# A planner that knows the array's tilings orders the routing, the mixtures and the last block

## The chip, the cores and the metric

The kernel runs on one core of a Trainium2 chip. The metric is the device time of one execution in microseconds (us), as the median of several runs.

## The reference, cut to what matters

Three residual blocks in float32 on 512 tokens of width 1024 (and, in the first block, 256 context tokens).

```python
# block 1: gated delta rule over 768 tokens, then a mixture of 16 experts
x, ctx = x + gate * gdn_mixer(norm(x), norm(ctx)), ...
x, ctx = x + gate * ec_moe(norm(x)), ctx + gate * ec_moe(norm(ctx))
# block 2: state-space mixer over 512 tokens, then a mixture of 16 experts
x = x + gate * ssd_mixer(norm(x), ...)
x = x + gate * ec_moe(norm(x))
# last block: three mixers side by side, then a gated feed-forward
h = rms_norm(x)
mixed = g0 * s5(h) + g1 * short_conv(h) + g2 * sparse_attention(h)
x = x + mixed @ w_out
x = x + (silu(h2 @ w_gate) * (h2 @ w_up)) @ w_down

def ec_moe(h, w_router, w_gate, w_up, w_down):   # every expert takes its best tokens
    aff = softmax(h @ w_router)
    gate, idx = top_k(aff.T, 2 * n // 16)        # 64 of 512 tokens, 32 of 256 context tokens
    xs = h[idx]
    y = (silu(xs @ w_gate[e]) * (xs @ w_up[e])) @ w_down[e] * gate
    return scatter_add(idx, y)
```

## The kernel before, in words

The kernel is written as a plain program of engine calls, but none of them is issued at once. A recorder (`Rec`) keeps each call with its engine, its operands, the calls it must follow (`preds`) and an estimated time (`cost`). At some dozen places `flush` turns the recorded calls into an order. `schedule` is a list scheduler: it keeps a clock for every engine (`free_at`), and again and again takes, over all engines, the ready call that can start first. Among the first 48 ready calls of an engine (`WINDOW`) the one with the best rank wins unless another starts more than `tol` ns earlier. The rank is the place in the program minus `beta` times the length of the chain that hangs on the call. `flush` runs `schedule` for every pair (`beta`, `tol`) in `trials`, takes the order with the shortest planned span, and issues it. That order is what each engine's queue holds on the chip, the queue of SyncE (SP), which issues all transfers, included. All this happens before the launch.

In the plan, a transfer costs its bytes at 360 per ns and transfers run one after the other. For TensorE the plan before has one row of matmuls, each holding the engine for its own cost. A matmul with 32 stationary columns, which occupies a quarter of the array, costs a quarter of a full one plus 27 ns; that four of them can run beside each other on four column strips, and that strips must be empty before the array is cut in another way, is not in the plan.

Which calls are where:

- First flush: norm of the input and the first part of the modulation (`ada`).
- `gdn`: the whole first mixer, its output projection and the logits of the first routing, one flush.
- `moe`, called with `two` true for the first mixture (tokens and context): one flush for softmax, top-k (`v.max`, `match_replace`), positions and the gather products `xs`, filled with two more rounds of `ada`; then one flush for the 16 experts. In the second mixture (tokens alone) there is a flush more after expert 5, and the preparation of the s5 mixer (`s5_prep`) rides in the rest.
- An expert: gate, up and context products (`eg`, `eu`, `ec`) from weight pieces `we` of 1 MB, each piece a transfer; the activation `eth`, `ct`; its transposes `hT` (tokens) and `hcT` (context); the down products `ey`, `eyc`; splits of the result into two parts (`yh`, `yl`, `ch`, `cl`). For every second expert `combine` spreads two experts' rows over the tokens: a matmul `pb` with 16 rows makes positions, VectorE compares (`pts`, one buffer), eight matmuls `po` follow, and VectorE adds each `po` pair to `X`. For every fourth expert the same is done for the context (`pbc`, `poc`).
- `ssd`: the second mixer (one flush), then its output projection and the second routing's logits (one flush).
- The last block: `s5` with the short convolution, `nsa` (the sparse attention: `sc` scores, `PT` transposes, `po` products with 64 columns, `hid` with 32 columns), `mix_out` and `ffn`, one flush each.

Stationary shapes: `eg`, `eu`, `ec`, `ey`, `eyc` of the first mixture are 128 rows by 32 columns; in the second mixture `eg`, `eu`, `ey` are 128 by 64; `hT`, `po`, `xs` are 128 by 128; `hcT` is 64 by 128; `pb`, `pbc` are 16 by 128. A float32 matmul appears in the trace as two MATMUL instructions; a 128-column one in the split number format as one.

All instructions of the program carry line 304 in the trace, the line of `flush` that issues them, so they are told apart by their tiles.

Of the kernel before, what the change touches and what calls it, by code (L numbers as in the profile page):

```python
# [11 lines left out]
F32 = mybir.dt.float32  # L12
F32R = mybir.dt.float32r
# [39 lines left out]
class Rec:  # L53
# [4 lines left out]
    def __init__(self, nc, tc):  # L58
        self.nc, self.tc = nc, tc
        self.tiles, self.ops = {}, []  # L60
        self.access = {}
        for e in ("tensor", "vector", "scalar", "gpsimd", "sync"):
            setattr(self, e, Proxy(self, e))
        self.free_at = {e: 0.0 for e in ("tensor", "vector", "scalar", "gpsimd", "sync")}
        self.dma_free = 0.0
        self.slot_times = {}
        self.seen = set()
        self.npool = 0
        self.run = None
        self.stacks, self.left = {"left": [], "right": []}, {"left": [], "right": []}  # L70
# [74 lines left out]
    def record(self, i, engine, method, a, k):  # L145
        reads, writes = [], []
        for j, x in enumerate(a):
            if isinstance(x, bass.AP):
                (writes if j == 0 else reads).append(x)
        for key, x in k.items():  # L150
            if isinstance(x, bass.AP):
                (writes if key in self.WRITES else reads).append(x)
        if method == "matmul" and not k.get("start", True):
            reads = reads + [writes[0]]
        preds = set()
        rr = [self.region(x) for x in reads]
        ww = [self.region(x) for x in writes]
        if engine != "tensor":
            rr, ww = ([r if not self.tiles.get(r[0], (0, 0, 0))[2] else (r[0], 0, 128) + r[3:] for r in z] for z in (rr, ww))
        for regs, wr in ((rr, False), (ww, True)):  # L160
            for r in regs:
                for (j, w2, q) in self.access.get(r[0], ()):
                    if (wr or w2) and j != i and q[1] < r[2] and r[1] < q[2] and q[3] < r[4] and r[3] < q[4]:
                        preds.add(j)
        for regs, wr in ((rr, False), (ww, True)):
            for r in regs:
                lst = self.access.setdefault(r[0], [])
                if wr:
                    lst[:] = [t for t in lst if not (r[1] <= t[2][1] and t[2][2] <= r[2] and r[3] <= t[2][3] and t[2][4] <= r[4])]
                lst.append((i, wr, r))  # L170
        if engine == "tensor":
            r = ww[0]
            key = r[0] + "#pe"
            q = (key, r[1] // 32 * 32, -(-r[2] // 32) * 32, 0, 1)
            lst = self.access.setdefault(key, [])
            preds.update(j for j, _, z in lst if j != i and q[1] < z[2] and z[1] < q[2])
            lst[:] = [t for t in lst if not (q[1] <= t[2][1] and t[2][2] <= q[2])]
            lst.append((i, True, q))
        names = {r[0] for r in rr + ww}
        cost = self.cost(engine, method, reads, writes, a, k)  # L180
        if i < len(self.ops):
            o = self.ops[i]
            o["preds"] |= preds
            o["names"] |= names
            o["cost"] += cost
            o["more"].append((method, a, k))
            return
        self.ops.append(dict(e=engine, m=method, a=a, k=k, preds=preds, names=names, cost=cost, psum=any(self.tiles.get(r[0], (0, 0, 0))[2] for r in rr + ww)))

    def cost(self, engine, method, reads, writes, a, k):  # L190
        def free(x):
# [48 lines left out]
    def latency(self, e, f):  # L240
        return self.LATENCY.get((e, f), 150.0)

    def flush(self, trials=((0.0, 30.0),)):

        ops = self.ops
        n = len(ops)
# [48 lines left out]
            t[o["e"]] = t.get(o["e"], 0.0) + (475.0 if "dma" in o["m"] else cost[i])  # L295
        static = succ, order, uses, conc, pos, size, tag, drain, tail, before
        best = min((self.schedule(static, *x) for x in trials), key=lambda r: r[0])
        self.span, self.seq, self.free_at, self.dma_free, times = best
        self.slot_times.update(times)
        self.seen.update(uses)  # L300
        for i in self.seq:
# [5 lines left out]
    def schedule(self, static, beta, tol):  # L307
# [13 lines left out]
        for t, lst in order.items():  # L321
            for nm in lst:
                if nm in self.seen:
                    got.add(nm)
                    slots[t].remove(max(slots[t]))
                    alloc[t].add(pos[nm])
                    nxt[t] = pos[nm] + 1
        npred = [len(o["preds"]) for o in ops]
        ready, end = [0.0] * n, [0.0] * n
        cand = {e: [] for e in free_at}  # L330
# [15 lines left out]
        while len(seq) < n:  # L346
            best = None
            for e, c in cand.items():
                fe = free_at[e]
                eb = None  # L350
                for r in c[: self.WINDOW]:
                    i = by[r]
                    st = max(fe, ready[i])
                    if eb is not None and st >= eb[0] - tol:
                        continue
                    for nm in ops[i]["tiles"]:
                        if nm in got:
                            continue
                        t = tag[nm]
                        if not free(nm) or (pos[nm] != nxt[t] and self.tiles[nm][2] and not drains(nm)):  # L360
                            break
                        st = max(st, min(slots[t]))
                    else:
                        if eb is None or st < eb[0] - tol:
                            eb = (st, r)
                            if st <= fe:
                                break
                if eb is not None and (best is None or eb < best[:2]):
                    best = eb + (e,)
            if best is None:  # L370
                return math.inf, seq, free_at, dma_free, slots
            st, r, e = best
            i = by[r]
            o = ops[i]
            cand[e].remove(r)
            for nm in o["tiles"]:
                if nm in got:
                    continue
                got.add(nm)
                t = tag[nm]  # L380
                slots[t].remove(min(slots[t]))
                alloc[t].add(pos[nm])
                ooo[t].add(pos[nm])
                while nxt[t] in alloc[t]:
                    ooo[t].discard(nxt[t])
                    nxt[t] += 1
            if "dma" in o["m"]:
                free_at[e] = st + 475.0
                dma_free = max(st + 1125.0, dma_free) + o["cost"] / 360.0
                fin = dma_free + 900.0  # L390
            else:
                fin = st + o["cost"]
                free_at[e] = fin
            end[i] = fin
            for nm in o["tiles"]:
                left[nm] -= 1
                if not left[nm]:
                    t = tag[nm]
                    slots[t].append(fin + 100.0)
                    ooo[t].discard(pos[nm])  # L400
            for j in succ[i]:
                npred[j] -= 1
                ready[j] = max(ready[j], fin + self.latency(e, ops[j]["e"]))
                if not npred[j]:
                    bisect.insort(cand[ops[j]["e"]], rank[j])
            seq.append(i)
        return max(end), seq, free_at, dma_free, slots


D = 1024  # L410
# [166 lines left out]
def gdn(K, H, apply, w, ba_w, conv_w, a_log, dt_b, norm_g, scr, bscr, tscr, rscr, side, xc, w_out, gate, route):  # L577
# [7 lines left out]

    nc, tc = K.nc, K.tc
    es = ExitStack()
    K.ring(es, 15)
    per = nc.pool(es, "gdn_per")
    live = nc.pool(es, "gdn_live")  # L590
# [352 lines left out]
            K.mm3(p, wt[:, d, :], last[:, t0:t1], True, True)  # L943
            v.scalar_tensor_tensor(X[:, d, t0:t1], p, gate(z)[:, d:d + 1], sums[d][:, t0:t1], op0=OP.mult, op1=OP.add)
    Rs = route(X, live.tile([128, 3, KT, 32], F32, name="router", tag="o", bufs=1))
    nc.flush(GDN_TRIALS)
    es.close()
    return X, Rs


GDN_TRIALS = ((0.4, 0.0),)
GDN_K = 128
GDN_V = 128

# [182 lines left out]
def moe(K, X, ws, regions, gate, routed, keep_next, gain, fill, side):  # L1137
# [153 lines left out]
    if two:  # L1291
        P0 += [places(0, 4, NE), places(1, 0, NE)]
        for k in range(KT):
            gather(k, P0)
            if 0 < k < 4:
                gates(*P0[k - 1])
    nc.flush(((0.0, 0.0),) if two else ((0.6, 30.0),))
    es.close()

    es = ExitStack()  # L1300
# [146 lines left out]
def ssd(K, H, apply, w, wz, w_dt, conv_w, conv_b, a_log, dt_b, d_skip, norm_g, w_out, gate, keep, scr, rscr, side, route):  # L1447
# [6 lines left out]
    nc = K.nc  # L1454
    v, s, g_, pe = nc.vector, nc.scalar, nc.gpsimd, nc.tensor
    es = ExitStack()
    K.ring(es, 18)
    per = nc.pool(es, "ssd_per")
    ssq = per.tile([128, TX], F32, name="ssq")
# [207 lines left out]
    for c in range(6):  # L1667
        scaled(c, Pair(low[:, 2 * c, :], low[:, 2 * c + 1, :]))
    nc.flush(((0.3, 30.0), (0.1, 0.0), (0.6, 0.0)))
    es1.close()  # L1670
    es2 = ExitStack()
    o = nc.pool(es2, "ssd_o")
# [23 lines left out]
        v.scalar_tensor_tensor(u, p, gate[:, d:d + 1], Rs, op0=OP.mult, op1=OP.mult)  # L1696
        v.tensor_tensor(X[:, d, 0:512], u, X[:, d, 0:512], op=OP.add)
    Rs = route(X, o.tile([128, 3, KT, 32], F32, name="router"))
    nc.flush(((0.6, 30.0), (0.8, 30.0), (0.8, 120.0)))
    es2.close()  # L1700
    es.close()
    return X, Rs
# [501 lines left out]
def mix_out(K, H, I, y5, yc, ya, keep, gain):  # L2204
# [41 lines left out]
        s.activation(H.hi[:, k, :], X[:, k, 0:512], AF.Copy, scale=gain[:, k:k + 1])  # L2246
        v.scalar_tensor_tensor(H.lo[:, k, :], X[:, k, 0:512], gain[:, k:k + 1], H.hi[:, k, :].bitcast(F32), op0=OP.mult, op1=OP.subtract)
    Rs = norm_stats(K, X, REGIONS_X)
    nc.flush(((0.6, 30.0),))
    es.close()  # L2250
    return X, Rs

# [4 lines left out]
def ffn(K, X, H, R, I, out):  # L2257
# [21 lines left out]
    for d in range(8):  # L2279
# [3 lines left out]
            K.mm3(p, wt[:, k, :], ht[k], k == 0, k == 21)  # L2283
        v.tensor_tensor(X[:, d, 0:512], p, X[:, d, 0:512], op=OP.add)
        nc.sync.dma_start(out[:, d, :], X[:, d, 0:512])
    nc.flush(((0.6, 30.0),))
    es.close()


def block2(K, X, Rs, I, scr, par, e_par, uscr, keep, out):  # L2290
# [21 lines left out]
    for half in range(2):  # L2312
        s5(K, H, I, y5[2 * half:2 * half + 2], scr, par[half], uscr, half, *pools)
        conv(2 * half)
        conv(2 * half + 1)
    nc.flush(((0.0, 30.0), (0.0, 60.0), (0.3, 60.0), (0.6, 60.0)))
    e2.close()
    e_par.close()
    b = nc.pool(e1, "b2a")
    ya = [b.tile([128, 512], F32, name=f"ya{i}") for i in range(4)]  # L2320
    e3 = nsa(K, H, I, ya)
    nc.flush(((1.0, 30.0),))
    e3.close()
    X, Rs = mix_out(K, H, I, y5, yc, ya, keep, ng[:, 1, :])
    e1.close()
# [195 lines left out]
```

## Time and profile before

| | |
|---|---|
| time, median of 3 runs | 3677.41 us (3665.22 to 3683.21) |
| profiled execution: its time | 3660.83 us |
| profiled execution: span from first to last instruction | 3659.1 us |
| TensorE busy | 3359.7 us, 92% of the span |
| VectorE, ScalarE, GpSimd busy | 51%, 32%, 15% |
| HBM traffic | 644.26 MB read, 21.30 MB written |
| mean granted TensorE clock | 0.971 |

The share of busy TensorE time is an upper figure: a strip of the array that works alone counts as a busy TensorE. Matmuls overlap in the records, so the time that one of them takes from the engine is read from the distance of starts, not from its own duration.

### The profile page before, as it was taken

The numbers are of one execution on the slowest core, as the hardware profiler recorded it, in microseconds if no ns is written. First come the engines' busy times: TensorE is split into PE (matmuls) and PEld (weight loads), VectorE is DVE, ScalarE is ACT, GpSimd is POOL, SyncE is SP. The second block draws the span as 40 slices with busy tenths as digits, with TensorE's granted clock in tenths as the row PEclk, the third lists the DMA queues.
The fourth block names the chain that finished last, engine by engine and source line by source line (L and its number), as shares of the span: only waits on it lengthen the run. The fifth ranks groups of instructions, "written<-read, shape, count | busy, mean of one in ns | idle before, by whom it ended". The sixth has DMA issues, their size and how long they took to land. (4 is left out here: it accounts for less than half of the span.)

```text
span 3659.1 us, 55424 instructions
## 1 busy us (share of the span) xinstructions
PE 3359.7 (92%) x21505; PEld 2255.5 (62%) x21505; DVE 1848.2 (51%) x4086; ACT 1181.0 (32%) x2518; POOL 555.4 (15%) x753
## 2 busy tenths in 40 slices
PE   7987979899999999899999879888879999999999
PEld 4776765666344444677877654332257658878887
DVE  4666755562223222778778542452164564445542
ACT  3354543423111111355555321120032353333331
POOL 0646544301000000013222010010011000000000
PEclk9999989899999999999999889999999999999999
DMA  5522227455888888354241359999962303333322
GB/s 188 160 60 56 74 65 230 155 188 197 342 312 311 335 317 315 111 147 133 93 141 53 140 220 401 362 368 421 420 143 81 119 1 98 96 100 92 96 87 87
DMA packets 251652, 669.21 MB, mean 183 GB/s; under 512 B 72156, under 2 KB 85612, under 8 KB 202236
## 3 DMA queue, kind: packets, MB, share of 16 engines
q1 hardware_dynamic: 251388, 665.66, 51.4%
q8 instruction: 169, 2.77, 0.3%
q14 instruction: 95, 0.78, 0.1%
HBM read 644.26 MB, written 21.30 MB: 182 GB/s over the span
## 5 line engine op out<-in xcount | busy, mean ns | idle before, releaser
L304 DVE TENSOR_TENSOR wl<-w,wh 128x512 fp32r<-128x512 f32 (+3 forms) x452 | 323.1, 717 | 458.8 <-PE fu L304 68.0
L304 ACT ACTIVATE wh<-w 128x512 fp32r<-128x512 f32 (+3 forms) x500 | 307.7, 622 | 675.2 <-PE fu L304 120.7
L304 PE MATMUL eg<-we,xs 128*32 128x512 f32 (+1 forms) x1536 | 371.5, 596 | 8.3 <-DMA we<-moe_w 7.2
L304 PE MATMUL eu<-we,xs 128*32 128x512 f32 (+1 forms) x1536 | 322.3, 595 | 7.4 <-DMA we<-moe_w 7.4
L304 PE MATMUL ey<-we,hTs 128*32 128x512 f32 (+1 forms) x1536 | 295.1, 601 | 17.2 <-ACT hTs L304 9.0
L304 PE MATMUL px<-H,wl 128*128 128x512 f32 (+1 forms) x768 | 269.3, 372 | 21.4 <-DVE wl L304 21.3
L304 PE MATMUL px<-H1l,wh 128*128 128x512 f32 (+1 forms) x768 | 267.3, 364 | 0.0
L304 PE MATMUL px<-H,wh 128*128 128x512 f32 (+1 forms) x768 | 266.1, 370 | 0.5 <-ACT wh L304 0.3
L304 PE MATMUL ec<-we,xs 128*32 128x512 f32 x1024 | 235.2, 594 | 0.0
L304 DVE TENSOR_TENSOR yl<-ey,yh 64x512 fp32r<-64x512 f32 x64 | 44.1, 689 | 337.8 <-ACT yh L304 337.3
L304 PEld LDWEIGHTS eg<-we,xs 128*32 128x32 f32 (+1 forms) x1536 | 96.3, 118 | 140.2 <-issue 103.9
L304 POOL TENSOR_TENSOR wl<-w,wh 128x512 fp32r<-128x512 f32 x48 | 64.6, 1346 | 761.7 <-DVE H1l L304 658.1
L304 DVE SCALAR_TENSOR_TENSOR eth<-eth,eg 128x512 f32<-128x512 f32 x32 | 22.0, 687 | 310.8 <-ACT eth L304 310.8
L304 PEld LDWEIGHTS eu<-we,xs 128*32 128x32 f32 (+1 forms) x1536 | 91.9, 119 | 141.1 <-issue 105.8
L304 PEld LDWEIGHTS ey<-we,hTs 128*32 128x32 f32 (+1 forms) x1536 | 97.3, 120 | 127.6 <-issue 61.8
L304 PEld LDWEIGHTS px<-H,wl 128*128 128x128 f32 x768 | 143.1, 192 | 43.8 <-DVE wl L304 26.2
L304 ACT ACTIVATE eth<-eg 128x512 f32<-128x512 f32 x32 | 19.1, 595 | 462.0 <-PE eg L304 404.7
L304 PEld LDWEIGHTS px<-H,wh 128*128 128x128 f32 x768 | 144.3, 192 | 25.0 <-issue 6.1
L304 PEld LDWEIGHTS px<-H1l,wh 128*128 128x128 f32 x768 | 142.9, 192 | 18.6 <-issue 1.3
L304 PE MATMUL eyc<-we,hcTs 128*32 128x256 f32 x1024 | 140.9, 379 | 0.0
L304 POOL TENSOR_TENSOR D<-D,x 48x30 f32<-48x30 f32 (+14 forms) x240 | 133.7, 557 | 18.3
L304 POOL TENSOR_TENSOR x<-D 48x30 f32<-48x30 f32 (+14 forms) x240 | 127.0, 529 | 59.4 <-DVE D L304 41.5
(1040 smaller groups left out, 7564.1 us busy)
## 6 DMA issues: line engine op xcount, KB each, us to landing
we<-moe_w SPq DMA_DIRECT2D x384, 1024.0 KB, 7.9
w<-ada_w SPq DMA_DIRECT2D x192, 256.0 KB, 5.2
w<-w_gu SPq DMA_DIRECT2D x88, 256.0 KB, 3.4
w<-gdn_w SPq DMA_DIRECT2D x64, 256.0 KB, 3.1
w<-ssd_w SPq DMA_DIRECT2D x64, 256.0 KB, 3.1
w<-w_mix SPq DMA_DIRECT2D x48, 256.0 KB, 2.7
w<-w_dn SPq DMA_DIRECT2D x40, 256.0 KB, 2.6
w<-ssd_wz SPq DMA_DIRECT2D x32, 256.0 KB, 2.6
```

The costliest lines, as they stand in the source:

```text
L304: getattr(getattr(self.nc, o["e"]), m)(*a, **k)
```

## The change

Nothing is added to or taken from the program that the chip runs; only the order of the calls is planned anew. `Rec.array` gives for each TensorE call its tiling (stationary rows and columns, rounded up to 32, 64 or 128), its place in that tiling, and the time that it holds that place. While the flag `plain` is false, `schedule` keeps the tiling that the array is in (`mode`), the time until which each place is held (`held`) and the time when all are done (`drained`). A call of the same tiling can start when its place is free, 7 ns behind the call before it; a call of another tiling starts 94 ns (`SWITCH`) after everything has drained. This state is handed from flush to flush. `plain` is set in `gdn` up to its end and in the first flush of `ssd`, which keep the plan as it was. The other flushes use fifteen pairs, `beta` in 0, 0.2, 0.4, 0.6, 1.0 with `tol` in 0, 30, 90, where they had one to four pairs before.

```diff
+    SWITCH = 94.0
+    @staticmethod
+    def array(method, a):
...
+        size = lambda x: 32 if x <= 32 else 64 if x <= 64 else 128
+        lhs, n = a[1], free(a[2])
+        rows, cols = size(lhs.ap[0][1]), size(free(lhs))
...
+        two = lhs.dtype == F32 and method != "transpose"
+        d = (2 if two else 1) * n / 2.4 + (13.5 if lhs.dtype == F32R else 4.0)
...
+        return (rows, cols), (r0 // rows, c0 // cols), (2 if two else 1) * d
...
-    def flush(self, trials=((0.0, 30.0),)):
+    TRIALS = tuple((b, t) for b in (0.0, 0.2, 0.4, 0.6, 1.0) for t in (0.0, 30.0, 90.0))
+    def flush(self, trials=TRIALS):
...
                     st = max(fe, ready[i])
+                    if e == "tensor" and not self.plain:
+                        tiling, place, _ = ops[i]["pe"][0]
+                        st = max(st, held.get(place, 0.0) if tiling == mode else drained + self.SWITCH)
...
+            elif e == "tensor" and not self.plain:
+                fin = at = st
+                for tiling, place, t in o["pe"]:
+                    if tiling != mode:
+                        if mode is not None:
+                            at = max(at, drained + self.SWITCH)
+                        mode, held = tiling, {}
+                    at = max(at, held.get(place, 0.0))
+                    held[place] = at + t
+                    drained = max(drained, at + t)
+                    fin = max(fin, at + t)
+                    at += 7.0
+                free_at[e] = max(at, held[place]) if mode == (128, 128) else at
...
 # gdn
+    nc.plain = True
...
-    nc.flush(GDN_TRIALS)
+    nc.flush(((0.4, 0.0),))
+    nc.plain = False
...
 # moe, first flush
-    nc.flush(((0.0, 0.0),) if two else ((0.6, 30.0),))
+    nc.flush()
...
 # ssd: plain for its first flush; then
-    nc.flush(((0.6, 30.0), (0.8, 30.0), (0.8, 120.0)))
+    nc.flush()
...
 # last block: mix_out and ffn (before: one pair each), s5 (four pairs), nsa
-    nc.flush(((0.6, 30.0),))
+    nc.flush()
...
-    nc.flush(((0.0, 30.0), (0.0, 60.0), (0.3, 60.0), (0.6, 60.0)))
+    nc.flush()
...
-    nc.flush(((1.0, 30.0),))
+    nc.flush()
```

## Rows read from the trace of the kernel before

**Rows 1.** Stretches of the span: busy us (x instructions), granted clock, DMA share, GB/s.

```profile
0.00:815.00 815.00, 701.30 (x5364) 530.20 (x5364) 488.38 (x1308) 338.13 (x802) 336.44 (x569) 0.94 0.43 132
815.00:870.00 55.00, 51.56 (x510) 40.99 (x512) 24.76 (x58) 30.27 (x80) 12.15 (x13) 0.97 0.06 20
870.00:1500.00 630.00, 615.16 (x5543) 276.37 (x5536) 179.97 (x387) 93.69 (x189) 0.29 (x2) 1.00 0.81 314
1500.00:2124.00 624.00, 570.89 (x3137) 475.98 (x3136) 460.45 (x901) 301.09 (x642) 137.48 (x98) 0.96 0.36 114
2124.00:2672.00 548.00, 473.09 (x2451) 194.56 (x2446) 201.95 (x453) 91.05 (x176) 46.02 (x34) 0.97 0.92 371
2672.00:2818.00 146.00, 126.32 (x816) 102.14 (x816) 81.73 (x155) 41.72 (x68) 23.02 (x38) 0.95 0.48 120
...
2893.00:3013.00 120.00, 111.20 (x575) 61.52 (x575) 80.56 (x235) 59.62 (x185) 0.00 (x0) 0.98 0.10 35
3013.00:3659.00 646.00, 637.04 (x2808) 519.57 (x2808) 286.97 (x439) 200.75 (x331) 0.00 (x0) 0.99 0.31 93
```

**Rows 2.** One slice inside the second mixture, same view and columns.

```profile
2561.00:2653.00 92.00, 77.46 (x334) 24.02 (x330) 16.83 (x26) 7.73 (x13) 0.00 (x0) 1.00 1.01 421
```

**Rows 3.** DMA issues of the page: the expert weights, KB each, us to landing.

```profile
we<-moe_w SPq DMA_DIRECT2D x384, 1024.0 KB, 7.9
```

**Rows 4.** TensorE groups, 870 to 1500 us: busy, mean ns, idle before.

```profile
L304 PE MATMUL ey<-we,hTs 128*32 128x512 f32 x1024 | 174.2, 594 | 6.0 <-DMA we<-moe_w 5.3 <-ACT hTs L304 0.8
L304 PE MATMUL eyc<-we,hcTs 128*32 128x256 f32 x1024 | 140.9, 379 | 0.0
L304 PE MATMUL po<-pts,yh 128*128 128x512 f32 x64 | 23.0, 420 | 1.0 <-ACT yh L304 0.9
```

**Rows 5.** TensorE in order of time, first mixture: start, us, operation, [idle before].

```profile
891.25 0.65 PE L304 MATMUL hT<-cst,eth 128*128 128x128 f32 x4
891.83 0.62 PE L304 MATMUL eg<-we,xs 128*32 128x512 f32 x1
...
893.68 0.46 PE L304 MATMUL hcT<-cst,ct 64*128 64x64 f32 x4
894.07 1.06 PE L304 MATMUL ey<-we,hTs 128*32 128x512 f32 x6
...
1095.55 1.04 PE L304 MATMUL ey<-we,hTs 128*32 128x512 f32 x8
1096.41 0.61 PE L304 MATMUL eyc<-we,hcTs 128*32 128x256 f32 x8
1096.84 0.60 PE L304 MATMUL eg<-we,xs 128*32 128x512 f32 x2
...
1097.90 1.21 PE L304 MATMUL po<-pts,yh 128*128 128x512 f32 x4
1099.33 1.20 PE L304 MATMUL po<-pts,yl 128*128 128x512 f32 x4 [0.21 <-DVE yl L304]
1100.46 0.39 PE L304 MATMUL pb<-posr,slp 16*128 16x512 bf16 x1
...
1498.55 0.39 PE L304 MATMUL poc<-pts,ch 128*128 128x256 f32 x1
```

**Rows 6.** VectorE group, 870 to 1500 us, same columns as rows 4.

```profile
L304 DVE SCALAR_TENSOR_TENSOR X<-po,mod,X 128x512 f32<-128x512 f32 x64 | 43.6, 743 | 1.1 <-PE po L304 0.7
```

**Rows 7.** TensorE in order of time, attention of the last block.

```profile
2893.45 1.05 PE L304 MATMUL hid<-w,A 128*32 128x256 f32 x4
2894.43 0.91 PE L304 MATMUL sc<-kz,qp 128*128 128x384 f32 x2
...
2947.33 1.07 PE L304 MATMUL po<-PT,vt 128*64 128x512 f32 x2
2948.34 1.20 PE L304 MATMUL PT<-cst,P 128*128 128x128 f32 x9
...
3003.30 2.78 PE L304 MATMUL po<-PT,vt 128*64 128x256 f32 x12
```

More of the change, by code (lines that the diff above doesn't have):

```diff
@@ L66, in __init__ @@
         self.slot_times = {}
+        self.array_at = None, {}, 0.0
+        self.plain = False
         self.seen = set()
@@ L180, in record @@
         cost = self.cost(engine, method, reads, writes, a, k)
+        pe = self.array(method, a) if engine == "tensor" else None
         if i < len(self.ops):
@@ L186, in record, with free @@
             o["more"].append((method, a, k))
+            o["pe"].append(pe)
             return
-        self.ops.append(dict(e=engine, m=method, a=a, k=k, preds=preds, names=names, cost=cost, psum=any(self.tiles.get(r[0], (0, 0, 0))[2] for r in rr + ww)))
+        self.ops.append(dict(e=engine, m=method, a=a, k=k, preds=preds, names=names, cost=cost, pe=[pe], psum=any(self.tiles.get(r[0], (0, 0, 0))[2] for r in rr + ww)))
+    SWITCH = 94.0
+    @staticmethod
+    def array(method, a):
+        def free(x):
+            n = 1
+            for s, c in x.ap[1:]:
+                n *= c
+            return n
+        size = lambda x: 32 if x <= 32 else 64 if x <= 64 else 128
+        lhs, n = a[1], free(a[2])
+        rows, cols = size(lhs.ap[0][1]), size(free(lhs))
+        r0, c0 = (x.offset // x.ap[0][0] % 128 if x.ap[0][0] else 0 for x in (lhs, a[0]))
+        wide = lhs.dtype in (F32, F32R)
+        two = lhs.dtype == F32 and method != "transpose"
+        d = (2 if two else 1) * n / 2.4 + (13.5 if lhs.dtype == F32R else 4.0)
+        if wide and cols == 128:
+            d = max(d, 109.0 * free(lhs) / 128 if lhs.dtype == F32 else 94.0)
+        elif wide:
+            d = max(d, 58.0 if cols == 64 else 30.0)
+        else:
+            d = max(d, 28.0)
+        return (rows, cols), (r0 // rows, c0 // cols), (2 if two else 1) * d
     def cost(self, engine, method, reads, writes, a, k):
@@ L297, in flush @@
         best = min((self.schedule(static, *x) for x in trials), key=lambda r: r[0])
-        self.span, self.seq, self.free_at, self.dma_free, times = best
+        self.span, self.seq, self.free_at, self.dma_free, times, self.array_at = best
         self.slot_times.update(times)
@@ L327, in schedule @@
                     nxt[t] = pos[nm] + 1
+        mode, held, drained = self.array_at
+        held = dict(held)
         npred = [len(o["preds"]) for o in ops]
@@ L370, in schedule @@
             if best is None:
-                return math.inf, seq, free_at, dma_free, slots
+                return math.inf, seq, free_at, dma_free, slots, None
             st, r, e = best
@@ L406, in schedule @@
             seq.append(i)
-        return max(end), seq, free_at, dma_free, slots
+        return max(end), seq, free_at, dma_free, slots, (mode, held, drained)
 D = 1024
@@ L945, in gdn @@
     Rs = route(X, live.tile([128, 3, KT, 32], F32, name="router", tag="o", bufs=1))
-    nc.flush(GDN_TRIALS)
+    nc.flush(((0.4, 0.0),))
+    nc.plain = False
     es.close()
     return X, Rs
-GDN_TRIALS = ((0.4, 0.0),)
 GDN_K = 128
@@ L1456, in ssd @@
     es = ExitStack()
+    nc.plain = True
     K.ring(es, 18)
@@ L1669, in ssd @@
     nc.flush(((0.3, 30.0), (0.1, 0.0), (0.6, 0.0)))
+    nc.plain = False
     es1.close()
@@ L2285, in ffn @@
         nc.sync.dma_start(out[:, d, :], X[:, d, 0:512])
-    nc.flush(((0.6, 30.0),))
+    nc.flush()
     es.close()
@@ L2321, in block2 @@
     e3 = nsa(K, H, I, ya)
-    nc.flush(((1.0, 30.0),))
+    nc.flush()
     e3.close()
```

## The prediction

> **What bounds the kernel now.** Read first the stretches of the span [rows 1]. No single engine bounds all of it. The mixers (0 to 815 us and 1500 to 2124 us) keep their plan, so the change speaks about the rest. From 870 to 1500 us, the first mixture, TensorE is busy for 615 of 630 us at the full granted clock of 1.00 (2.4 GHz), while the DMA engines are busy for 0.81 of the time at 314 GB/s: TensorE sets the end there. From 2124 to 2672 us, the routing of the second block and the second mixture, the DMA share is 0.92 and TensorE is busy for 473 of 548 us; a late slice runs at a share of 1.01 and 421 GB/s [rows 2]. The weights set the end there: of 384 pieces of 1024 KB [rows 3] half belong to this mixture, 192 x 1.049 MB = 201 MB, which at 421 GB/s take 478 us. From 2893 to 3013 us, most of the attention, TensorE is busy for 111 of 120 us, VectorE for 81. From 3013 us on TensorE is busy for 637 of 646 us in runs of one tiling; order has nothing to give there.
>
> Busy is not full, though. Look next at the starts of TensorE's instructions in the first mixture [rows 5]. From 1095.55 to 1096.41 us eight `ey` take 0.86 us: four 32-column strips work side by side, and one instruction costs 0.1075 us. Eight `eyc` take 0.43 us, 0.054 each. But the twelve instructions between 891.83 us, behind the transposes `hT`, and 893.68 us, where `hcT` starts, take 1.85 us where full strips would take 12 x 0.1075 = 1.29. A visit to another tiling leaves the strips partly filled before and behind it, 0.56 us in this case.
>
> Now add up the stage. `eg`, `eu`, `ec` and `ey` are 1024 instructions each, `eyc` 1024 (two of the groups stand in [rows 4]): 4096 x 0.1075 = 440 us and 1024 x 0.054 = 55 us. 128 `po` at most (1100.46 - 1097.90) / 8 less the idle, 0.29 us each [rows 5]: 37 us. `hT` 0.58 and `hcT` 0.39 us per expert, 16 experts: 16 us. The 167 others (`poc`, `pb`, `pbc`, the norm) at most 0.15 each, which is the price of one `hT`: 25 us. Sum 573. Of the 57 us that are left to 630, some 8 are idle time (6.0 before `ey` and 1.0 before `po`, [rows 4]). About 49 us are strips that stand empty. In the timeline from 870 to 1500 us I count 69 visits away from the 32-column tiling and back, the first the `hT` at 891.25, the last the `poc` at 1498.55 [rows 5]: 0.7 us each, and about 0.1 more for the change of tiling itself that a merged visit saves. I take 0.8 us a visit.
>
> **The change, part by part.** No instruction is added or removed, and the planning happens before the launch, so every term is one of order.
>
> First mixture. The plan before had no notion of strips and took a ready call of lower rank at once, so `hT` and `hcT` of one expert go out 2.4 us apart with twelve products between them [rows 5], and `pb` alone. In the new plan a call of another tiling can start only when all places have drained, up to 0.86 us later, plus 94 ns; any product whose weights are there starts earlier and wins. So calls of other tilings pile up until the products run dry, and go out in fewer visits: `hT` with `hcT`, `pb` with the `po` of the other half. Per four experts this merges four visits of `hcT` into those of `hT` and about three of the nine visits of `pb`, `po`, `pbc` and `poc`. I take 28 of the 69: 28 x 0.8 = 22 us. Bounds: none merge, 0; two visits per expert remain, 37 x 0.8 = 30, and with the idle time 38. Below zero: if the planner splits visits, ten more cost 8 us.
>
> What queues behind: `hT` waits longer, so `hTs` and with it `ey` come later, three pieces of down weights stay in their buffers, and SP's queue, which is issued in plan order, waits on them. The DMA share of 0.81 covers that: an expert's 12.6 MB take 30 us at 421 GB/s, and the stage has 39 us per expert. Without that cover it is a rival below.
>
> Evictions may set the pace inside a merged visit. VectorE needs 743 ns to add a `po` pair to `X` [rows 6]; a pair takes TensorE 2 x 0.29 = 0.58 us. The four pairs of one visit hide this in free PSUM buffers; with the two halves of `combine` merged all the way, 16 halves would wait for 4 x (0.743 - 0.58) = 0.65 us each, 10 us, and this part would give 12 instead of 22. I keep 22, because a visit that stalls on a PSUM buffer is one that the new plan leaves for the strips, and take the 12 as a rival.
>
> The Trainium skill, "TensorEngine Tiling (Array Packing)", PSUM Bottleneck, speaks for the lower figure: packing speeds up TensorE but not the evacuation of PSUM, which may become the bound. By that rule this part is -12, by the rows of the visits as they are now -22; that the eviction of a pair is the slower of the two here, 743 ns against 580, agrees with it.
>
> Attention. From 2893 to 3013 us I count 39 visits away from the full array, the first the `hid` at 2893.45, the last the `po` at 3003.30 [rows 7]. Two `po` instructions, one matmul on one half of the array, take 1.01 us (2947.33 to 2948.34); two such matmuls on both halves would take the same. I count 17 such lone visits. `hid` with four instructions takes 0.98 us and fills two of four strips in part. Merging lone `po` in pairs ends 8 visits at about 0.8 us (the shorter ones cost less than 1.01), and three visits of `hid` end at 0.98: 6.4 + 2.9, I take 10 with the tails. Bounds: 0, because the softmax chain may force the order, and half of all visits at 0.8, 16.
>
> Second mixture. TensorE works here on 64-column halves and waits for pieces; fewer changes give nothing while weights set the end, and that wait is the cover. The mean of 371 GB/s [rows 1] against 421 [rows 2] leaves 548 - 203/0.421 = 66 us in which transfers are not at full rate, mostly before the first expert (its routing is a chain of VectorE that no tiling shortens) and beside `s5_prep`. A new order can give some of it back or lose more. I take -3, between -15 and +12, a fifth of the 66 on either side.
>
> s5 and convolution, 2672 to 2818 us: TensorE idles or drains for 20 of 146 us in chains of other engines; -2, between -5 and +4. Gather of the first mixture, 815 to 870 us, busy 51.6 of 55: -1, between -3 and +2. `mix_out` and `ffn`: 9 us idle of 646: 0, between -4 and +2. The mixers: same costs, ranks and trials, but the planner starts them from other engine clocks; no row shows what that does, 0, with 4 us either way as an estimate, half a per cent of a mixer.
>
> Sum: -22 - 10 - 3 - 2 - 1 = -38 us. The profiled execution took 3660.8 us; 3622.8 is 0.990 of it. The median of the runs, 3677.4, is 1.0045 of the profiled one, so the forecast is 3639 us.
>
> **The rivals.** *The plan sees gaps that the chip has not.* The plan moves weights at 360 per ns: an expert's 12 pieces take 12 x 1.049 MB / 360 = 35.0 us. Its TensorE work by the rows is 573/16 = 35.8. The two are so close that the plan may have TensorE wait for almost every piece, and in a planned gap a visit costs nothing, so it stays a visit of its own. On the chip the pieces come at 421 and the visits cost their 0.8 us. Then the mixture gives 5 or less and the rest 10: 3646 of the profiled execution, -15 us, 3662. For it speaks the closeness; against it, that planned work is still the larger of the two.
>
> *Delayed transposes hold the weights.* If products of expert e+1 run until they are dry before `hT` of e goes out, its down pieces hold their three buffers for eight pieces of 24 instructions, about 8 x 2.6 = 21 us, and SP stands at the fourth. The stage has 39.4 - 29.9 = 9.5 us per expert to make up for a stop. From a stop of 9.5 us on, TensorE waits for weights: 13 us would cost 3.5 x 16 = 56 us, net +18 with the 38 saved, 3679 of the profiled execution, 3695. For it: `ey` already has 5.3 us of waits for `we` [rows 4], and the second mixture has less slack still. Against: buffers of the gate and up pieces are others than those of the down pieces, so transfers go on around a stop that the plan has foreseen.
>
> *The evictions bind.* The variant by 743 ns against 580 above: -28 in all, 3649.
>
> **How the numbers follow.** A difference under 0.5% (18 us) can't be told from none with this kernel. The forecast, -18 to -78, has 0.60, the bound evictions 0.06 of the same sign, and 0.03 goes to more than -78. The planned gaps with less than 18 us either way have 0.19, held weights 0.12. So faster 0.69, same 0.19, slower 0.12. Low end: -38 - 16 (mixture) - 6 (attention) - 12 - 3 - 2 - 4 (the others at their bounds) = -81, of which -76 is kept because not all come together: 3585 x 1.0045 = 3601. The high end takes in the planned gaps and stops short of the held weights: 3684.
>
> **What would show it.** Count the visits from `eg` to the end of the first mixture: 41 rather than 69, with `hcT` right behind `hT`, and the stage 608 us rather than 630. In the attention few `po` x2 between `PT`, 110 us rather than 120. The second mixture's length should stay within 15 us at about 370 GB/s. The forecast is wrong if visits stay near 69 (planned gaps), if idle time before `ey` or `eg` for `we` grows past 50 us (held weights), or if a mixer with an unchanged plan moves by more than 5 us.

## The result, and the profile after

The changed kernel takes 3612.65 us as the median of four runs (3608.77 to 3614.22), beside 3673.55 us for the kernel before (3665.22 to 3683.21, four runs): a ratio of 0.9832, 95% interval 0.9804 to 0.9859. The profiled executions span 3612.4 and 3659.1 us, 46.7 apart. The medians are 60.9 apart: the profiled execution before was the shortest of its kernel, that of the changed kernel the longest of its own, so the stages below add up to the 46.7. The time lies inside the range, and the gain is larger than the forecast 38 by either measure.

Stretches of the span of the changed kernel, cut at the same events as [rows 1]; columns as there:

```profile
0.00:817.00 817.00, 707.01 (x5368) 534.43 (x5368) 489.40 (x1309) 339.26 (x804) 336.72 (x569) 0.94 0.42 132
817.00:870.00 53.00, 48.80 (x472) 40.44 (x476) 22.75 (x50) 28.88 (x79) 11.99 (x12) 0.95 0.02 4
870.00:1479.00 609.00, 594.24 (x5580) 224.15 (x5576) 181.18 (x394) 91.97 (x190) 0.49 (x2) 0.99 0.84 328
1479.00:2099.00 620.00, 571.25 (x3152) 476.56 (x3153) 461.46 (x901) 301.04 (x641) 136.98 (x98) 0.96 0.35 113
2099.00:2638.00 539.00, 463.04 (x2454) 192.12 (x2439) 201.79 (x453) 93.04 (x178) 44.56 (x34) 0.96 0.93 377
2638.00:2783.00 145.00, 122.75 (x824) 100.11 (x816) 84.62 (x158) 41.91 (x69) 22.84 (x38) 0.91 0.48 121
...
2863.00:2966.00 103.00, 92.05 (x534) 59.92 (x535) 80.54 (x238) 57.93 (x183) 0.00 (x0) 0.96 0.04 14
2966.00:3612.40 646.40, 636.38 (x2808) 518.81 (x2807) 288.36 (x439) 199.75 (x331) 0.00 (x0) 0.99 0.30 93
```

The first mixture went from 630 to 609 us, the routing and mixture of the second block from 548 to 539, the part of the attention shown from 120 to 103. The stretch in front of that part, not shown, grew from 75 to 80, since all of `hid` now stands there (40 of its 64 instructions stood behind the first `sc` before). The rest moved by 4 us or less. Measured between fixed events instead of round times, first `eg` to the last norm row `nm_R`: 638.6 to 616.8 us; first `eg` of the second mixture to the first `u`: 532.8 to 522.0; first `q` product to the first `br`: 194.3 to 182.0, of which 120.2 to 102.6 behind the first `sc`. These three measures are used below, as stage 1, stage 2 and attention (behind `sc`). Each is read from one execution. The experiment e9 below plans the first two blocks as the kernel before does, and its stage 1 is 2.8 us shorter and its stage 2 3.8 us longer; smaller differences than that say nothing.

TensorE in order of time, first mixture, the changed kernel:

```profile
964.65 1.46 PE L335 MATMUL ec<-we,xs 128*32 128x512 f32 x8
966.04 0.50 PE L335 MATMUL po<-pts,yh 128*128 128x512 f32 x1
...
967.78 0.39 PE L335 MATMUL po<-pts,yl 128*128 128x512 f32 x1
968.01 0.60 PE L335 MATMUL hT<-cst,eth 128*128 128x128 f32 x4
968.54 0.39 PE L335 MATMUL pb<-posr,slp 16*128 16x512 bf16 x1
968.86 0.46 PE L335 MATMUL hcT<-cst,ct 64*128 64x64 f32 x4
969.30 1.06 PE L335 MATMUL ey<-we,hTs 128*32 128x512 f32 x8
...
1084.47 0.28 PE L335 MATMUL pbc<-posr,slp 16*128 16x256 bf16 x1
1085.36 1.92 PE L335 MATMUL eu<-we,xs 128*32 128x512 f32 x16 [0.61 <-DMA we<-moe_w]
...
1093.20 0.28 PE L335 MATMUL pbc<-posr,slp 16*128 16x256 bf16 x1
1094.05 0.39 PE L335 MATMUL poc<-pts,ch 128*128 128x256 f32 x1 [0.58 <-DVE pts L335]
```

The first visit shown holds eight `po`, `hT`, `pb` and `hcT`, the merging that was forecast; ten of the visits in stage 1 are of this kind. There are 29 visits away from the 32-column tiling instead of 70 (69 in the prediction's count). The eight `po` take 1.97 us, from 966.04 to 968.01, and wait for no eviction. But TensorE now also stands inside visits: between `pbc` at 1093.20 and `poc` at 1094.05 it is idle for 0.58 us and waits for `pts`.

In the attention, the visits with 64 columns are few and long (same view, changed kernel):

```profile
2900.11 4.53 PE L335 MATMUL po<-PT,vt 128*64 128x512 f32 x32
2921.82 4.53 PE L335 MATMUL po<-PT,vt 128*64 128x512 f32 x32
2936.03 4.52 PE L335 MATMUL po<-PT,vt 128*64 128x512 f32 x28
```

Thirty-two instructions, of 128 to 512 columns, take 4.5 us, where [rows 7] show two of 512 columns in 1.01.

### The profile page after: what moved, and what is told of

Read it like the earlier page. It is cut to its first block, busy times and chain, and to the rows that moved or that the text cites. A ratio compares the mean times of both kernels' runs of the same rounds, so it can differ in the third digit from the quotient of the medians.

```text
span 3612.4 us, 55450 instructions
## 1 busy us (share of the span) xinstructions
PE 3314.7 (92%) x21505; PEld 2200.4 (61%) x21505; DVE 1850.2 (51%) x4086; ACT 1177.9 (33%) x2518; POOL 553.6 (15%) x753
## 5 line engine op out<-in xcount | busy, mean ns | idle before, releaser
L335 PE MATMUL eg<-we,xs 128*32 128x512 f32 (+1 forms) x1536 | 288.7, 599 | 7.3 <-DMA we<-moe_w 6.2
L335 PE MATMUL eu<-we,xs 128*32 128x512 f32 (+1 forms) x1536 | 258.5, 597 | 9.1 <-DMA we<-moe_w 9.1
L335 PE MATMUL ey<-we,hTs 128*32 128x512 f32 (+1 forms) x1536 | 244.3, 601 | 12.8 <-ACT hTs L335 9.0
L335 PE MATMUL ec<-we,xs 128*32 128x512 f32 x1024 | 175.3, 592 | 0.0
L335 PEld LDWEIGHTS eg<-we,xs 128*32 128x32 f32 (+1 forms) x1536 | 75.8, 119 | 148.1 <-issue 123.0
L335 PEld LDWEIGHTS eu<-we,xs 128*32 128x32 f32 (+1 forms) x1536 | 70.4, 119 | 155.0 <-issue 128.2
L335 PEld LDWEIGHTS ey<-we,hTs 128*32 128x32 f32 (+1 forms) x1536 | 69.3, 120 | 146.7 <-issue 110.8
L335 POOL TENSOR_TENSOR D<-D,x 48x30 f32<-48x30 f32 (+14 forms) x240 | 134.2, 559 | 18.3
L335 ACT ACTIVATE yh<-ey 64x512 fp32r<-64x512 f32 x64 | 37.9, 592 | 257.0 <-PE ey L335 242.5
```

The costliest lines, as they stand in the source:

```text
L335: getattr(getattr(self.nc, o["e"]), m)(*a, **k)
```

## The experiments

Three theories were put against each other. A is the prediction's: each visit to another tiling costs about 0.8 us, and the plan saves visits. B: the wider search of fifteen pairs finds better orders by itself. C came after the first four runs: not the visit costs, but a broken four, four products for the four strips between which something else is issued, so that strips stand empty; a visit between whole fours costs little.

In the table, stage 1 and the attention are in us, visits are leaves of the 32-column tiling (stage 1) or of the full array (attention), "fours" is the share of the 5120 expert instructions whose starts come four together, less than 20 ns apart, and "idle" is time in stage 1 in which no matmul ran, each counted from the starts in the trace.

| kernel | stage 1 | visits | fours | idle | stage 2 | attention | visits | whole, ratio to before |
|---|---|---|---|---|---|---|---|---|
| before | 638.6 | 70 | 38% | 19.5 | 532.8 | 120.2 | 40 | 1 |
| changed | 616.8 | 29 | 86% | 19.4 | 522.0 | 102.6 | 8 | 0.9832 (0.9804 to 0.9859) |
| e1 pairs of beta, tol alone | 639.8 | 70 | 47% | 19.9 | 564.7 | 118.6 | 40 | 1.0062 (1.0041 to 1.0083) |
| e2 tilings, old pairs | 627.4 | 30 | 87% | 24.7 | 533.9 | 104.9 | 8 | 0.9922 (0.9903 to 0.9942) |
| e3 change free | 599.7 | 68 | 100% | 15.5 | 533.6 | 100.7 | 22 | 0.9874 (0.9851 to 0.9898) |
| e5 fours, plan of before | 616.1 | 70 | 100% | 24.4 | 539.3 | 118.6 | 40 | 0.9924 (0.9899 to 0.9949) |
| e6 change free in stage 1 | 605.9 | 65 | 97% | 14.8 | 520.9 | 100.9 | 8 | 0.9821 (0.9795 to 0.9846) |
| e7 fours, changed plan | 601.8 | 41 | 99.7% | 18.3 | 522.1 | 102.6 | 8 | 0.9828 (0.9814 to 0.9843) |
| e8 change at 600 ns in stage 1 | 641.4 | 29 | 95% | 42.5 | 519.9 | 101.0 | 8 | 0.9924 (0.9903 to 0.9944) |
| e9 pairs in the attention, plan of before | 635.8 | 70 | 38% | 17.2 | 536.6 | 107.5 | 30 | 0.9947 (0.9927 to 0.9966) |
| e10 transfers at 421 | 644.5 | 29 | 60% | 44.4 | 526.1 | 100.0 | 9 | 0.9939 (0.9918 to 0.9960) |
| e11 fours, change free | 608.6 | 76 | 99.8% | 14.5 | 521.2 | 101.0 | 8 | 0.9830 (0.9811 to 0.9850) |

### Search or tilings (e1, e2)

```diff
 # e1: the plan never uses the tilings; the fifteen pairs stay
-        self.plain = False
+        self.plain = True
 # e2: the tilings stay; every flush has its pairs of before, e.g.
-    nc.flush()
+    nc.flush(((0.0, 0.0),) if two else ((0.6, 30.0),))
```

> The fifteen pairs of beta and tol are kept, the tilings are taken out of the plan everywhere. Theory A (the plan's knowledge of strips and drains merges visits): the first mixture stays near 630 us with 60 or more visits away from the 32-column tiling, the attention near 120 us, the whole kernel within 0.5% of before. Theory B (the wider search finds the better orders by itself): the first mixture near 605 us, the attention near 108, the whole near 3612 us.

> The tilings stay in the plan, but every flush has the one to four pairs of the kernel before. Theory A: first mixture 605 to 612 us with about 30 visits, attention 108 to 113 us, the whole 3610 to 3630 us. Theory B: first mixture 620 to 632 us, the whole 3650 to 3675 us.

B falls with e1. The pairs alone leave stage 1 and the attention where they were and make the whole kernel slower, by 0.6%. The place is stage 2: 564.7 us instead of 532.8. With the old pairs the tilings keep 11 of the 22 us in stage 1 and 15 of the 18 in the attention. In stage 2 neither half gives anything alone; together they give 11 us. But e2 did not come out as A said either: its 30 visits are A's, its 627.4 us lie in B's range, the attention (104.9) is below A's, and the whole (3644.58 us) lies between the two. Its stage 1 has as many whole fours and visits as that of the changed kernel and is 10.6 us longer, of which 5.3 are idle time.

### The price of a change (e3)

```diff
-    SWITCH = 94.0
+    SWITCH = 0.0
```

> The 94 ns for a change of tiling are set to 0 in the plan; that all places must drain first stays in it. Theory A1 (the drain of up to 0.86 us is what makes visits wait): first mixture within 5 us of 604, 28 to 40 visits. Theory A2 (the price of 94 ns decides): 50 visits or more and 615 to 630 us; the attention, where many calls use the full array and nothing is left to drain, back to 112 us or more.

This was expected to tell what makes the plan hold visits back. It did (68 visits: the 94 ns hold them back, as A2 said), but stage 1 came out at 599.7 us, the fastest of all, with as many visits as before. A2's time was wrong by 15 us or more, and so was its attention (112 us or more expected, 100.7 measured); A1's visits were wrong. So the number of visits can't be what 22 us hang on, and theory C was formed: here every four is whole.

### Whole fours in either plan (e5, e7)

```diff
     def product(p, x, w, i, first, last):
         if two:
-            for j in range(4):
+          with nc.together():
+            for j in range(4):
...
 # the same around the four products of ec and the four of eyc
```

> The kernel before, its plan untouched, but the four products that belong on the four column strips are recorded as one call in the first mixture, so that nothing can come between them. Theory A (the number of visits to other tilings costs): about 70 visits stay and the first mixture stays within 8 us of 639 (from the first eg to the last norm row). Theory C (what costs are broken fours: a visit or another product between the four leaves strips empty, a visit at a whole four costs 0.3 us): 598 to 612 us with about 70 visits.

> The changed kernel with the four products recorded as one call in the first mixture. Theory A: 29 visits or so already taken out, so 610 to 618 us. Theory C: 597 to 606 us, nearly all starts in fours, at whatever number of visits.

e5 is the cleanest run of the study. The plan is that of before, it knows no strips, it makes 70 visits as before; only the fours can't be broken. Stage 1 takes 616.1 us, as long as in the changed kernel, 22.5 us less than before. TensorE in order of time in e5, the place of [rows 5]:

```profile
888.79 0.66 PE L304 MATMUL hT<-cst,eth 128*128 128x128 f32 x4
889.38 1.06 PE L304 MATMUL ec<-we,xs 128*32 128x512 f32 x8
890.26 1.04 PE L304 MATMUL ey<-we,hTs 128*32 128x512 f32 x8
891.23 0.46 PE L304 MATMUL hcT<-cst,ct 64*128 64x64 f32 x4
891.62 1.06 PE L304 MATMUL ey<-we,hTs 128*32 128x512 f32 x8
```

Between `hT` and `hcT` lie 1.85 us, as in [rows 5]; but sixteen instructions fit in, not twelve. Full strips would take 16 x 0.1075 = 1.72 us, so the visit costs its neighbours 0.13 us, not 0.56. C expected 598 to 612 us. What may explain the 4 us above that are waits, which the groups of TensorE in stage 1 of e5 name:

```profile
L304 PE MATMUL ey<-we,hTs 128*32 128x512 f32 x1024 | 137.6, 610 | 13.4 <-DMA we<-moe_w 12.6 <-ACT hTs L304 0.8
```

With the products faster, `ey` waits 12.6 us for weights instead of the 5.3 of [rows 4]. One of these waits shows that a wait can cost more than its own length. TensorE in order of time in e5, and TensorE's busy time, granted clock, DMA share and GB/s of a stretch inside it:

```profile
1055.14 1.84 PE L304 MATMUL ey<-we,hTs 128*32 128x512 f32 x8 [1.98 <-DMA we<-moe_w]
1056.74 1.10 PE L304 MATMUL eyc<-we,hcTs 128*32 128x256 f32 x8
1057.59 1.60 PE L304 MATMUL ey<-we,hTs 128*32 128x512 f32 x8
...
1055.30:1058.70 3.40, 3.40 (x24) 0.50 1.01 422
```

Behind the wait of 1.98 us the granted clock stood at 0.50 (1.2 GHz) for 3.4 us, and eight `eyc` took 0.85 us instead of the 0.43 of [rows 5]. In stage 1 TensorE was busy for 14.9 us at this lower level in e5, for 5.8 us in the kernel before and for 13.0 in the changed one.

e7, the fours in the changed plan, comes to 601.8 us, as C said.

### Fewer or more visits at will (e6, e8, e11)

```diff
 # only while the experts of the first mixture are planned
+    nc.SWITCH = 0.0 if two else 94.0    # e6, e11 (with the fours of e7); 600.0 in e8
     nc.flush()
+    nc.SWITCH = 94.0
```

> The changed kernel with the 94 ns set to 0 only while the experts of the first mixture are planned. Theory A: more visits than 29, so more than 617 us. Theory C: 596 to 604 us with 60 to 70 visits, routing as in the changed kernel, the whole 3590 to 3602 us.

> The changed kernel with the 94 ns raised to 600 only while the experts of the first mixture are planned. Theory A: fewer than 29 visits and 605 to 616 us. Theory C: no gain from fewer visits, 615 to 630 us, as more calls wait inside a visit for one another.

> The changed kernel with the four products of the first mixture recorded as one call and the 94 ns set to 0 while its experts are planned: theory C's version, which should beat both kernels. First mixture 596 to 603 us; the whole 3592 to 3606 us against 3612 of the changed kernel. Theory A: 610 us or more, no better than the changed kernel.

In e6 stage 1 is shorter with 65 visits than that of the changed kernel with 29: 605.9 against 616.8 us, 2 us above what C said; the whole, 3607.17 us, misses C's 3590 to 3602. In e8 the plan is made to avoid changes still harder. It doesn't get below 29, loses 25 us against the changed kernel and is back at the length of before. C said 615 to 630, so the loss is larger than either theory gave. Its idle time is 42.5 us, and TensorE was busy for 31 us at the lower clock. The groups of TensorE in stage 1 of e8 show a part of the idle time:

```profile
L335 PE MATMUL po<-pts,yh 128*128 128x512 f32 x64 | 28.6, 447 | 7.7 <-DVE slp L335 5.7 <-DVE pts L335 2.0
...
L335 PE MATMUL poc<-pts,ch 128*128 128x256 f32 x32 | 10.8, 356 | 11.6 <-DVE pts L335 11.6
```

The same group in the changed kernel, and in the kernel before, where there was little of it:

```profile
L335 PE MATMUL poc<-pts,ch 128*128 128x256 f32 x32 | 10.7, 358 | 7.7 <-DVE pts L335 7.7
...
L304 PE MATMUL poc<-pts,ch 128*128 128x256 f32 x32 | 10.3, 343 | 2.1 <-DVE pts L304 2.1
```

`pb` or `pbc`, the comparison `pts` on VectorE and `po` or `poc` are a chain. A plan that avoids changes keeps TensorE in the visit until the comparison is there: 11.6 us of `poc` in e8, 7.7 in the changed kernel, 2.1 before. A plan that changes freely goes back to the products in between (2.8 us in e6, 3.6 in e11).

e11 joins e6 and e7 and was to beat both kernels. Its stage 1 of 608.6 us misses the expected 596 to 603, its whole of 3610.65 us the 3592 to 3606, and stage 1 is slower than e7's 601.8 with 76 visits instead of 41. Without idle time e11 needs 594.1 and e7 583.5 us. But that is not the price of 35 visits, since e3, with 68, needs only 584.2. The granted clock tells e3 and e11 apart (stage 1 of each, columns of [rows 1]):

```profile
880.40:1480.20 599.80, 584.35 (x5563) 210.76 (x5562) 186.20 (x407) 96.53 (x193) 0.49 (x2) 1.00 0.86 333
874.80:1483.40 608.60, 594.09 (x5577) 211.36 (x5578) 187.37 (x413) 96.30 (x194) 0.43 (x2) 0.99 0.85 330
```

TensorE was busy at the lower level for 2.6 us in e3, 12.7 in e7 and 16.0 in e11. To leave this out, take the stretches of expert products between two visits, without idle time and with half of the time at the lower level (products take twice as long there, see e5), less 0.1075 us for each instruction (0.054 for `eyc`). What remains is an estimate of the time in which strips stand empty: 43 us before, 21 in the changed kernel, 12 in e5, 10 in e11, 8 in e3, 5 in e7. The last round in front of a visit holds 0.2 us of it per visit in e3, e5, e7 and e11 alike, where the fours are whole, and 0.33 before. So where the fours are whole anyway, a visit costs about 0.2 us. As wholes, e6, e7 and e11 (0.9821, 0.9828, 0.9830) can't be told from the changed kernel (0.9832).

### The attention (e9)

```diff
-                for h in range(2):
-                    pe.matmul(po[64 * h:64 * h + 64, kt * 128:512], ...)
+                with nc.together():
+                  for h in range(2):
+                    pe.matmul(po[64 * h:64 * h + 64, kt * 128:512], ...)
...
 # the same around the two strips of hid
```

> The kernel before, its plan untouched, but in the attention the two halves of every po product, and the two strips of every hid product, are recorded as one call. Theory C (lone halves cost, not visits): the attention from the first sc to the first br falls from 120 us to 104 to 112 us, with visits still 25 or more. Theory A (visits): it falls only as far as visits fall, at 0.8 us each, and the rest comes from merging: 112 to 119 us.

107.5 us with 30 visits, in the plan of before: 12.7 of the changed kernel's 17.6 us without any knowledge of tilings. From the first `q` product on, where `hid` counts wherever it stands, e9 takes 178.7 us, 15.6 less than before; the changed kernel gains 12.3 there. TensorE in order of time in e9:

```profile
2956.43 1.08 PE L304 MATMUL po<-PT,vt 128*64 128x512 f32 x4
2957.44 0.28 PE L304 MATMUL sc<-mneg,idb 128*128 128x128 bf16 x2
```

Four instructions on both halves take 1.01 us, the time of two on one half in [rows 7].

### Transfers at the measured rate (e10)

```diff
-                dma_free = max(st + 1125.0, dma_free) + o["cost"] / 360.0
+                dma_free = max(st + 1125.0, dma_free) + o["cost"] / 421.0
 # and in the chain lengths
```

> The changed kernel with the plan's transfer rate raised from 360 to the measured 421 per ns. If the second mixture's 9 us came from the tilings: it stays within 6 us of 522 (first eg to first u). If it is the choice among orders whose planned lengths hardly differ while the plan believes the transfers to be the bound: a plan with the true rate chooses otherwise, 500 to 515 us, or a move of 10 us or more in either direction. The first mixture stays within 8 us of 617, since there the plan is already bound by TensorE.

Stage 2 stays, 526.1 us. Stage 1, which was to stay, goes from 616.8 to 644.5. What TensorE waits for there:

```profile
PE eg L335 <- DMA we<-moe_w: 10.4, 12, 2.1
PE eu L335 <- DMA we<-moe_w: 9.9, 7, 2.4
PE ey L335 <- DMA we<-moe_w: 7.5, 7, 3.7
```

27.8 us of waits for weights, where the changed kernel's groups show about 3. That a plan which trusts the measured peak of [rows 2] puts the products behind pieces that come later than it thinks is argued, not tried. Fewer fours start together, too (60%), but this costs next to nothing here: without idle time e10 needs 600.1 us and the changed kernel 597.4, with 29 visits in both, and the strips stand empty for 21 us in both. TensorE in order of time in e10 shows how:

```profile
995.92 0.60 PE L335 MATMUL ec<-we,xs 128*32 128x512 f32 x2
995.99 0.60 PE L335 MATMUL eg<-we,xs 128*32 128x512 f32 x2
996.35 0.60 PE L335 MATMUL ec<-we,xs 128*32 128x512 f32 x2
996.42 0.60 PE L335 MATMUL eg<-we,xs 128*32 128x512 f32 x2
```

The strips start two by two, 0.07 us apart, and a round of four instructions still takes 0.43 us. A four that does not start together is not yet an empty strip.

### The mixers (e4, e12)

```diff
 # e4: gdn and ssd
-    nc.plain = True
 # e12: gdn and ssd
-    nc.plain = True
+    nc.SWITCH = 0.0
```

> The two mixers get the tilings too, with their own pairs of beta and tol as they were. If the knowledge is worth as much there (about 250 changes of tiling, most between full array and parts of it), each mixer gains 5 to 15 us and the whole comes to about 3595 us. If their chains of other engines set the end, a call held back for its tiling delays a chain: each mixer loses 3 to 15 us, the whole 3620 to 3640 us.

> The tilings in the plan of the two mixers as well, but with the 94 ns set to 0 there. If the mixers lost 72 and 20 us because a call that wants another tiling is put off for any call that does not: up to the first eg 865 to 890 us and the second mixer within 5 us of 513. If they lost because the plan prices small matmuls and their chains otherwise: still 920 us or more up to the first eg.

With the tilings in the mixers' plan the kernel takes 3709.13 us, 1.0105 (1.0085 to 1.0124) of before, far outside both expectations: 942 us up to the first `eg` instead of 870, and 533 instead of the changed kernel's 513 in the second mixer. e12 shows that it isn't the 94 ns: without them the first `eg` comes at 969 us, the second mixer takes 532, and the whole 3732.13 us, in a single run. What in the tilings' prices misleads the plan there was not found.

## Why the prediction came out as it did

- **First mixture, -22 us predicted, -21.8 measured, by another mechanism.** The step that failed is "69 visits [...] 0.7 us each, and about 0.1 more for the change of tiling itself that a merged visit saves. I take 0.8 us a visit." The empty strips were real, 43 us by the count above; they were booked on the visits because a visit is where the eye meets them, the twelve instructions of [rows 5]. Twelve is not a whole number of eights (a four, each float32 product in two instructions): it was the broken four that cost 0.56 us, and the same visit at a whole four costs 0.13 in e5. The count was off too, 41 visits fewer rather than 28. At 0.8 us they would have given 33; at about 0.2 us they are 8, of which the new waits for `pts` take back 5.6 (7.7 less 2.1). That the rest is from fours that are no longer broken, by a visit or between visits (38% to 86% start together), is argued from e5, which binds the fours, keeps the 70 visits and gains as much; no run splits the changed kernel's own gain. That a wrong count times a wrong price came within 0.2 us of the measured time is luck.
- **Attention, -10 predicted, -12.3 measured** from the first `q` product on, -17.6 behind `sc` less 5.3 in front of it, where all of `hid` now stands. The step was right in kind: lone halves. It was again mostly the half and not the visit (e9). Only the size was off: the visits end nearly all, 40 to 8, not 11 of 39.
- **Second mixture, -3 predicted, -10.8 measured** (-9 over the prediction's stretch, which takes in the routing), inside the bounds of -15 and +12. In the 105 us in which `s5_prep` runs beside the experts the DMA share rose from 0.89 to 0.97, first the kernel before, then the changed one:

```profile
2332.00:2437.00 105.00, 87.24 (x393) 33.93 (x391) 72.58 (x221) 20.86 (x35) 21.11 (x13) 0.95 0.89 346
...
2308.00:2413.00 105.00, 92.38 (x426) 38.86 (x428) 76.69 (x225) 27.87 (x44) 20.91 (x13) 0.92 0.97 382
```

  36 GB/s more than before's 346 over 105 us are 3.8 MB, 9 us at 421 GB/s. It needs the tilings at 94 ns and the fifteen pairs together: e1, e2 and e3, which lack one of these, stand at 533 us or far above, the other seven kernels with both at 520 to 523 and e10, whose transfers are planned faster, at 526. Which instruction of `s5_prep` holds the weights up less is open.
- **The small terms.** Gather -1 predicted, -1.2 measured, with the routing in front of it; s5 -2 and -0.5; `mix_out` and `ffn` 0 and +0.8; the mixers 0, and +1.8 before the first mixture and -1.8 in the second, within the 4 us allowed. The second mixer's output projection, with -2.0, had no term; the routing behind it took 1.2 more.
- **The rivals.** Planned gaps: no, the visits fell to 29. Held weights: no, `ey` waits 1.9 us for `we`, 5.3 before. That rival was real at another point: e10 shows 27.8 us of such waits once the plan believes in faster transfers. Evictions: no. Eight `po` run in 1.97 us, and no visit holds more of them, so the 16 in a row for which the prediction counted 10 us did not come. The Trainium skill ("TensorEngine Tiling (Array Packing)", PSUM Bottleneck) has it that the evacuation of PSUM may become the bound once tiling speeds up TensorE; TensorE waits for none in this stage of the changed kernel.

## What to carry to other kernels

Where small matmuls share the array, look at the starts: whether every strip gets its instruction in each round says more than how often the tiling changes. Before a planner is taught the array, bind the products that belong together; that gave 22 us in the first mixture here with the old plan, and 12.7 of 17.6 in the attention. More trials are only worth as much as the plan that judges them: with the old plan fifteen pairs cost 0.6%.

## What the runs showed of the hardware that was not expected

A change of tiling between whole fours costs the products beside it 0.13 us, and about 0.2 us a visit on the mean of stage 1, in four kernels with 41 to 76 visits (e3, e5, e7, e11; an estimate, idle time and the lower clock taken off). A wait of 2 us for weights cost more than itself: behind it the granted clock fell to 0.50 for 3.4 us, and the products took twice as long (e5). In the second mixture weights arrive at 421 GB/s, yet a plan that counts on this rate for pieces of 1 MB leaves TensorE waiting 27.8 us in the first mixture, while a plan at 360 leaves it waiting 3.
